# A hybrid attention layer with 32 experts: the output projection as three float32r passes

## The chip, the cores and the metric

The kernel runs as one program on one core of a Trainium2 chip. A core has TensorE (PE, matrix products; PEld is its loading of weights), VectorE (DVE), ScalarE (ACT), GpSimd (POOL) and SyncE (SP, which here issues most of the transfers), working memory of 128 partitions (SBUF), accumulators for products (PSUM), and 16 DMA engines that fetch from HBM. The metric is the device time of one execution in microseconds (us); lower is better.

## The reference

One layer on 256 rows of 1,024 channels, in float32. What surrounds the change, cut to its lines:

```python
merged = (gates[:, :, 0] * (y_a @ w_branch_a[l])
          + gates[:, :, 1] * (y_b @ w_branch_b[l])
          + gates[:, :, 2] * (y_c @ w_branch_c[l]))
mix = merged @ w_out[l]                                  # 256x1024 @ 1024x1024
x = _layer_norm(DEEPNORM_ALPHA * x + mix, ln1_g[l], ln1_b[l])
ffn = _moe(x, w_router[l], b_router[l], w_up[l], b_up[l], w_down[l], b_down[l])
x = _layer_norm(DEEPNORM_ALPHA * x + ffn, ln2_g[l], ln2_b[l])
```

`y_a`, `y_b`, `y_c` are the outputs of the attention, of the pooling and of the state space branch; all three and the gates come from one input projection `x @ w_in`. In `_moe` each row goes to 4 of 32 experts; an expert has 12 MB of weights, so that all of them are 384 MB.

## The kernel before, in words

Two parts follow each other. The **trunk** is everything up to the first layer norm and the router. The **experts** follow, two at a time, in 16 pairs of 24 weight chunks.

**The ring.** All large weights come through a ring of `NW` = 22 slots of 128x2048 float32 (1 MB each). Chunks 0 to 28 are the trunk's (`wt`), the 384 behind them the experts' (`wm`). A slot serves for other things too: the pieces of `x`, the gates (`gates0` to `gates2`), the branch outputs (`y`), `z` for the layer norm, and three slots `f_spl` for weights that are taken apart. `done` gives a chunk's slot back, `release` any other, and `load_more` (L109) at once writes a transfer of the next chunk into the program on SP's queue. SP carries these out in the order in which they were written: a transfer waits until its slot is free, and all behind it wait too. At most eight transfers are under way; a further one waits for the one eight places earlier. The ring is full when 22 slots are taken; it then loads no faster than the products give slots back.

**Three passes.** The products of the gates, of `v` and of the pooling input are done in float32r, which keeps part of a float32 number's bits. `split_next` takes a half chunk (128x1024) apart: ScalarE copies it rounded (`hi`, L233), VectorE subtracts (`lo`, L234). Then three products replace one in float32: hi by hi, hi by lo and lo by hi. The list `jobs` sets the order in which halves are taken apart, always up to three ahead, in the three slots `f_spl` in turn.

**The end of the trunk.** After the last gate product, `branch(d)` (d = 0 to 7) makes 128 of the 1,024 merged channels: eight float32 products of 256 columns (L768) into `pab` and `pcc`, then VectorE multiplies by the gates and adds (L777, L778, L782), and L783 writes `m`. `mixk` then adds channel block k to the output projection: four float32 products of 512 columns (L789), for two blocks of rows `t` and two halves of the columns `n`, into four accumulators `mix[t][n]` that gather over k. The weights of a branch pair and of an output pair come in chunks 21 to 28 in turn. The order on TensorE is written out in the code: `branch(k + 1)` stands ahead of `mixk(k)`, so that VectorE has a whole group of products' time for `m`:

```python
    branch(0)
    for k in range(7):
        branch(k + 1)
        if k < 6:
            mixk(*[(k, t, n) for t in range(2) for n in range(2)])
    mixk((6, 0, 0), (6, 0, 1), (6, 1, 0), (7, 0, 0), (7, 0, 1), (6, 1, 1), (7, 1, 0), (7, 1, 1))
```

(Left out there: small steps for the router between the groups.) Then L839 adds the residual to each accumulator, the rows are transposed (L851), and the router picks the experts (L866 to L952). The first product of an expert pair is L1037 (its bias), those with weights are L1028; `done` follows every four of them.

In a trace a float32 product shows as two records of TensorE, a float32r product as one.

Of the kernel before, what the change touches and what calls it, by code (L numbers as in the profile page):

```python
# [7 lines left out]
F32 = mybir.dt.float32  # L8
F32R = mybir.dt.float32r
BF16 = mybir.dt.bfloat16  # L10
I32 = mybir.dt.int32
ACTF = mybir.ActivationFunctionType
ALU = mybir.AluOpType
# [4 lines left out]
S = 256  # L18
# [36 lines left out]
CH_V = [6, 7]  # L55
CH_UP = 8
CH_G = list(range(9, 21))
CH_BR = [21, 23, 25, 27]
CH_WO = [22, 24, 26, 28]
N_TRUNK = 29  # L60


@with_exitstack
def hybrid_layer(ctx: ExitStack, tc: tile.TileContext, wt, wm, pa, pb, pc, xin, bu, lnp, b_down, out):
    nc = tc.nc
    pe, act, dve, pool, sp = nc.tensor, nc.scalar, nc.vector, nc.gpsimd, nc.sync
    TT, TS, STT = dve.tensor_tensor, dve.tensor_scalar, dve.scalar_tensor_tensor

    con = ctx.enter_context(tc.tile_pool(name="con", bufs=1))
# [5 lines left out]

    n_chunks = N_TRUNK + NP * 24
    chunks = {}
# [41 lines left out]
    def chunk(i):  # L119
        return chunks[i][0]  # L120

    def done(i):
        f = chunks.pop(i)[1]
        release(f)
# [17 lines left out]
    ones32 = con.tile([128, 32], F32)  # L142
    epst = con.tile([128, 2], F32)
    hpi = con.tile([128, 1], F32)
    junk = con.tile([128, 1], F32)


    ph1 = ExitStack()
# [55 lines left out]
    def drop(name):  # L204
        release(big.pop(name)[1])


    def gate_tile(i, n=1):
        return big[f"gates{i // 8}"][0].rearrange("p (u t) -> p u t", u=8)[:, i % 8:i % 8 + n]

    def yv(k, n=1):
        return big["y"][0].rearrange("p (k t) -> p k t", k=8)[:, k:k + n]
# [3 lines left out]

    SPLIT = CH_V + [CH_UP] + CH_G
    jobs = [(c, h) for c in SPLIT for h in range(2)]  # L220
    js = {"emitted": 0, "used": 0}
    parts = {}

    def split_next():
        j = js["emitted"]
        if j >= len(jobs):
            return
        js["emitted"] += 1
        ci, h = jobs[j]
        src = chunk(ci)[:, h * 1024:(h + 1) * 1024]  # L230
        t = place(f_spl[j % 3], F32R)
        hi, lo = t[:, 0:1024], t[:, 1024:2048]
        act.activation(out=hi, in_=src, func=ACTF.Copy)  # L233
        TT(lo, src, hi.bitcast(F32), op=ALU.subtract)  # L234
        parts[j] = (hi, lo)
        if h:
            done(ci)

    def split(ci, h):
        j = js["used"]  # L240
        js["used"] += 1
        assert jobs[j] == (ci, h)
        while js["emitted"] <= j:
            split_next()
        return parts.pop(j)

    def mm3(out, whi, wlo, ahi, alo, first, last):
        pe.matmul(out, whi, ahi, start=first, stop=False)  # L248
        pe.matmul(out, whi, alo, start=False, stop=False)  # L249
        pe.matmul(out, wlo, ahi, start=False, stop=last)  # L250
# [146 lines left out]


    def proj(ci, half, dst):
        if ci in SPLIT:  # L400
            hi, lo = split(ci, half)
            for k in range(8):
                mm3(dst, hi[:, k * 128:(k + 1) * 128], lo[:, k * 128:(k + 1) * 128], xhi[:, k], xlo[:, k], k == 0, k == 7)
            split_next()
        else:
            w = chunk(ci)[:, half * 1024:half * 1024 + 1024]
            for k in range(8):
                pe.matmul(dst, w[:, k * 128:(k + 1) * 128], xt3[:, k], start=(k == 0), stop=(k == 7))  # L408
            if half:
                done(ci)  # L410

    def pair_tile():
        return pm.tile([128, 2, S], F32, tag="m", name="pm")
# [190 lines left out]

    pus = pair_tile()
    proj(CH_US, 0, pus[:, 0])
    proj(CH_US, 1, pus[:, 1])
    act.activation(out=usT, in_=pus, func=ACTF.Copy)
    forget_logits()
# [131 lines left out]
    ph1.close()  # L741
    release(f_xhi)
    release(f_xlo)
    for f in f_spl:
        release(f)


    late = ctx.enter_context(tc.tile_pool(name="late", bufs=1, reuse_waits="tile"))
# [9 lines left out]
    wk2 = ps2.enter_context(tc.tile_pool(name="wk2", bufs=2, reuse_waits="tile"))  # L758
    mix = [[pmx.tile([128, 512], F32, name=f"mix{t}{n}") for n in range(2)] for t in range(2)]
    mst = {}  # L760

    def branch(d):
        w = chunk(CH_BR[d // 2])[:, d % 2 * 1024:d % 2 * 1024 + 1024]
        pab = pbr.tile([128, 2, S], F32, tag="ab", name="pab")
        pcc = pbr.tile([128, S], F32, tag="c", name="pcc")
        for dst, k0, k1 in ((pab[:, 0], 0, 4), (pab[:, 1], 4, 6), (pcc, 6, 8)):
            for k in range(k0, k1):
                pe.matmul(dst, w[:, k * 128:(k + 1) * 128], yv(k)[:, 0], start=(k == k0), stop=(k == k1 - 1))  # L768
        if d % 2:
            done(CH_BR[d // 2])  # L770

        t = wk2.tile([128, 3, S], F32, tag="mg", name="mg")
        if d == 5:
            STT(t[:, 0:1], gate_tile(15), 1.0, pab[:, 0:1], op0=ALU.add, op1=ALU.mult)
            STT(t[:, 1:2], gate_tile(16), 1.0, pab[:, 1:2], op0=ALU.add, op1=ALU.mult)
        else:
            STT(t[:, 0:2], gate_tile(3 * d, 2), 1.0, pab, op0=ALU.add, op1=ALU.mult)  # L777
        STT(t[:, 2:3], gate_tile(3 * d + 2), 1.0, pcc[:, None], op0=ALU.add, op1=ALU.mult)  # L778
        if d in (2, 5, 7):
            drop(f"gates{(d - 1) // 3 if d > 2 else 0}")  # L780
        m = wk2.tile([128, S], F32, tag="m", name="m", bufs=3)
        TT(t[:, 0], t[:, 0], t[:, 1], op=ALU.add)  # L782
        TT(m, t[:, 0], t[:, 2], op=ALU.add)  # L783
        mst[d] = m

    def mixk(*parts):
        for k, t, n in parts:
            w = chunk(CH_WO[k // 2])[:, k % 2 * 1024 + n * 512:k % 2 * 1024 + n * 512 + 512]
            pe.matmul(mix[t][n], mst[k][:, t * 128:(t + 1) * 128], w, start=(k == 0), stop=(k == 7))  # L789
            if (k % 2, t, n) == (1, 1, 1):  # L790
                done(CH_WO[k // 2])


    def router_weights():
# [15 lines left out]
    for k in range(7):  # L810
# [14 lines left out]
        if k < 6:  # L825
            mixk(*[(k, t, n) for t in range(2) for n in range(2)])
    mixk((6, 0, 0), (6, 0, 1), (6, 1, 0), (7, 0, 0), (7, 0, 1), (6, 1, 1), (7, 1, 0), (7, 1, 1))


    ps3 = ExitStack()  # L830
# [5 lines left out]
    for t in range(2):  # L836
        for n in range(2):
            ns = slice(n * 512, (n + 1) * 512)
# [57 lines left out]
    for t in range(2):  # L896
        for n in range(2):
            ns = slice(n * 512, (n + 1) * 512)
# [445 lines left out]
```

## Time and profile before

| | us |
|---|---|
| median of 3 runs | 1161.49 (1161.32 to 1161.6) |
| the profiled execution | 1161.53 |
| its span, first to last instruction | 1159.8 |
| TensorE busy | 1130.4 (97%) |
| TensorE's weight loads busy | 527.4 (45%) |
| VectorE busy | 300.9 (26%) |
| ScalarE busy | 184.7 (16%) |
| moved by DMA | 438.05 MB, mean 378 GB/s |

The profiled execution stands 0.04 us above the median, and 1.7 us of it lie outside the span. The busy share of TensorE is no measure of what bounds the kernel, since matmuls overlap and a matmul that waits for data in the pipeline counts as busy. The page's 40 slices of 29 us each show the moved GB/s over time; the views by stage show which engine waits for what.

### The profile page before, as it was taken

Reading aid. Unit: us, or ns where it says so; the run is one execution under the profiler, and the core shown is the slowest. Engines: PE = TensorE matmul, PEld = TensorE weight load, DVE = VectorE, ACT = ScalarE, POOL = GpSimd, SP = SyncE. Lnnn points to the kernel's source line nnn. Section 1 sums busy time; section 2 is a strip of 40 time slices with the busy share of each in tenths; the row PEclk is TensorE's granted clock in tenths of the full one; section 3 lists DMA queues with packets and bytes.
Section 4 is the critical chain, followed back from the end, with each engine's and each line's share of the span. In section 5 each row is a group of like instructions: output and inputs, shape, how many; then the busy total and the mean of one; then the engine's idle time right before and its main releaser. Section 6 shows DMA issues by size and latency. Waiting matters only on the chain. (4 is left out here: it accounts for less than half of the span.)

```text
span 1159.8 us, 13362 instructions
## 1 busy us (share of the span) xinstructions
PE 1130.4 (97%) x5535; PEld 527.4 (45%) x5535; DVE 300.9 (26%) x710; ACT 184.7 (16%) x389; POOL 13.5 (1%) x19
## 2 busy tenths in 40 slices
PE   9999999999999999999999999999999999999996
PEld 6888986643434343434343433343434344334332
DVE  4798622430202111111212121111111111111042
ACT  4555410310101010101010101010101010101002
POOL 0000000000000000000000000000000000000100
PEclk9999999999999999999999999999999999999999
DMA  9733685699999999999999999999999999999992
GB/s 368 306 110 137 243 358 212 253 423 421 420 421 421 421 421 421 421 421 420 421 422 420 421 421 420 414 422 420 422 421 420 422 420 421 421 421 420 420 412 87
DMA packets 63169, 438.05 MB, mean 378 GB/s; under 512 B 7136, under 2 KB 7648, under 8 KB 10752
## 3 DMA queue, kind: packets, MB, share of 16 engines
q1 hardware_dynamic: 62064, 435.46, 91.2%
q10 hardware_dynamic: 864, 1.54, 0.4%
q8 instruction: 45, 0.74, 0.3%
q0 software_dynamic: 176, 0.15, 0.0%
q14 instruction: 20, 0.16, 0.0%
HBM read 436.07 MB, written 1.05 MB: 377 GB/s over the span
## 5 line engine op out<-in xcount | busy, mean ns | idle before, releaser
L1028 PE MATMUL hu<-w,xg 128*64 128x512 f32 x2048 | 480.9, 596 | 14.2 <-DMA w<-in_wm_dram 14.2
L1028 PEld LDWEIGHTS hu<-w,xg 128*64 128x64 f32 x2048 | 166.0, 137 | 316.0 <-issue 262.1
L1028 PE MATMUL py<-w,at 128*64 128x512 f32 x1024 | 231.5, 597 | 0.0
L1000 DVE TENSOR_SCALAR s<-hu 128x256 f32<-128x256 f32 x64 | 27.0, 422 | 581.6 <-PE hu L1028 581.6
L1028 PEld LDWEIGHTS py<-w,at 128*64 128x64 f32 x1024 | 70.5, 136 | 136.0 <-issue 129.6
L1011 ACT ACTIVATE at<-pta 128x256 f32<-128x256 f32 x64 | 24.5, 383 | 422.9 <-PE pta L1010 422.9
L1037 PE MATMUL hu<-bup,pc_sb 128*64 128x512 f32 x256 | 68.3, 605 | 0.0
L1017 PE MATMUL acc<-y,gT 128*128 128x512 f32 x128 | 63.5, 618 | 1.5 <-ACT y L1045 1.5
L248 PE MATMUL pm<-w,w 128*128 128x256 f32 x208 | 60.6, 291 | 0.8 <-ACT vsb L641 0.8
L965 PE MATMUL pg<-oh,x 128*128 128x128 f32 x512 | 59.9, 275 | 0.0
L249 PE MATMUL pm<-w,w 128*128 128x256 f32 x208 | 58.8, 283 | 0.0
L250 PE MATMUL pm<-w,w 128*128 128x256 f32 x208 | 58.8, 282 | 0.0
L965 PEld LDWEIGHTS pg<-oh,x 128*128 128x128 f32 x512 | 58.4, 192 | 0.1
L1001 ACT ACTIVATE hu<-s 128x256 f32<-128x256 f32 x64 | 24.6, 385 | 168.3 <-DVE s L1000 168.3
L1045 ACT ACTIVATE y<-py 128x512 f32<-128x512 f32 x32 | 19.1, 597 | 190.9 <-PE py L1028 190.9
L234 DVE TENSOR_TENSOR w<-w,w 128x1024 fp32r<-128x1024 f32 x30 | 36.5, 1219 | 19.3 <-ACT w L233 19.1
L248 PEld LDWEIGHTS pm<-w,w 128*128 128x128 f32 x208 | 39.7, 191 | 3.8 <-issue 1.7
L1017 PEld LDWEIGHTS acc<-y,gT 128*128 128x128 f32 x128 | 21.7, 189 | 42.9 <-issue 39.7
L249 PEld LDWEIGHTS pm<-w,w 128*128 128x128 f32 x208 | 39.8, 191 | 0.1
L250 PEld LDWEIGHTS pm<-w,w 128*128 128x128 f32 x208 | 39.8, 191 | 0.0
L233 ACT ACTIVATE w<-w 128x1024 fp32r<-128x1024 f32 x30 | 31.6, 1057 | 35.3 <-PE pm L250 25.1
L408 PE MATMUL pm<-w,w 128*128 128x256 f32 x160 | 36.1, 383 | 1.1 <-DMA w<-in_wt_dram 1.1
(320 smaller groups left out, 681.8 us busy)
## 6 DMA issues: line engine op xcount, KB each, us to landing
w<-in_wm_dram SPq DMA_DIRECT2D x382, 1024.0 KB, 19.8
w<-in_wt_dram SPq DMA_DIRECT2D x26, 1024.0 KB, 7.9
w<-in_wm_dram SPq DMA_DIRECT2D x8, 256.0 KB, 11.7
w<-in_wt_dram SPq DMA_DIRECT2D x4, 256.0 KB, 5.6
w<-in_wt_dram ACTq DMA_DIRECT2D x4, 256.0 KB, 5.9
w<-in_wt_dram SPq DMA_DIRECT2D x2, 512.0 KB, 5.0
w<-in_xin_dram SPq DMA_DIRECT2D x1, 1024.0 KB, 7.7
w<-in_pb_dram SPq DMA_DIRECT2D x1, 896.0 KB, 8.5
```

What stands on the lines that cost most here:

```text
L233: act.activation(out=hi, in_=src, func=ACTF.Copy)
L234: TT(lo, src, hi.bitcast(F32), op=ALU.subtract)
L248: pe.matmul(out, whi, ahi, start=first, stop=False)
L249: pe.matmul(out, whi, alo, start=False, stop=False)
L250: pe.matmul(out, wlo, ahi, start=False, stop=last)
L408: pe.matmul(dst, w[:, k * 128:(k + 1) * 128], xt3[:, k], start=(k == 0), stop=(k == 7))
L965: pe.matmul(pg[:, b], x1[:, t, k * 128:(k + 1) * 128], oh[:, t], start=(t == 0), stop=(t == 1))
L1000: TS(xg, hu[:, 0:256], 7.0, None, op0=ALU.min)
L1001: act.activation(out=th, in_=xg, func=ACTF.Tanh, scale=0.851)
L1017: pe.matmul(accs[t][n], gT[:, t * 128:(t + 1) * 128], y, start=first, stop=True, skip_group_check=True)
L1028: pe.matmul(dst[64 * e:64 * e + 64], lhs[:, k, 64 * e:64 * e + 64], w[:, k % 4], start=first and k == 0, stop=(k == 7))
L1037: pe.matmul(hu[64 * e:64 * e + 64], ident[:, i:i + 1].to_broadcast([128, 64]), bup, start=True, stop=False)
```

## The change

The output projection's weights (chunks 22, 24, 26, 28) join the list `jobs`, behind those of the gates, so that `split_next` takes their eight halves apart too. `branch` no longer writes `m`: it adds in place, ScalarE copies the sum rounded to `mh` (128x256, float32r) and VectorE subtracts to `ml`. `mixk` does three float32r products for each of its float32 products, and calls `split_next` after the last of a block. A chunk's slot now goes back when its second half has been taken apart (`half_done`), not when it has been multiplied. The three slots `f_spl`, which went back after the gates, go back after the last `mixk`. Last, a tile of 96 bytes takes the place of one of 4 (which took 32), ahead of the ring: in the built program the ring starts at byte 20,416 of a partition before, and at 20,480 = 20 x 1,024 now. The branch products stay in float32 (the loop's `d in ()` holds for none).

```diff
-    junk = con.tile([128, 1], F32)
+    scr = con.tile([128, 24], F32)
+    junk = scr[:, 0:1]
...
-    SPLIT = CH_V + [CH_UP] + CH_G
-    jobs = [(c, h) for c in SPLIT for h in range(2)]
+    jobs = [(c, h) for c in CH_V + [CH_UP] + CH_G for h in range(2)]
+    for d in range(8 + LAG):
...
+        if d - LAG in (0, 1, 2, 3, 4, 5, 6, 7):
+            jobs.append((CH_WO[(d - LAG) // 2], (d - LAG) % 2))
...
+    def half_done(ci):
+        halves[ci] = halves.get(ci, 0) + 1
+        if halves[ci] == 2:
+            done(ci)
...
-    for f in f_spl:
-        release(f)
...
-        m = wk2.tile([128, S], F32, tag="m", name="m", bufs=3)
         TT(t[:, 0], t[:, 0], t[:, 1], op=ALU.add)
-        TT(m, t[:, 0], t[:, 2], op=ALU.add)
-        mst[d] = m
+        if (CH_WO[d // 2], d % 2) in jobs:
+            mh = wk2.tile([128, S], F32R, tag="mh", name="mh", bufs=3)
+            ml = wk2.tile([128, S], F32R, tag="ml", name="ml", bufs=3)
+            TT(t[:, 0], t[:, 0], t[:, 2], op=ALU.add)
+            act.activation(out=mh, in_=t[:, 0], func=ACTF.Copy)
+            TT(ml, t[:, 0], mh.bitcast(F32), op=ALU.subtract)
+            mst[d] = mh, ml
...
     def mixk(*parts):
         for k, t, n in parts:
-            w = chunk(CH_WO[k // 2])[:, k % 2 * 1024 + n * 512:k % 2 * 1024 + n * 512 + 512]
-            pe.matmul(mix[t][n], mst[k][:, t * 128:(t + 1) * 128], w, start=(k == 0), stop=(k == 7))
-            if (k % 2, t, n) == (1, 1, 1):
-                done(CH_WO[k // 2])
...
+                if k not in ws:
+                    ws[k] = split(ci, h)
+                hi, lo = ws[k]
+                pe.matmul(mix[t][n], m[:, ts], hi[:, ns], start=(k == 0), stop=False)
+                pe.matmul(mix[t][n], m[:, ts], lo[:, ns], start=False, stop=False)
+                pe.matmul(mix[t][n], ml[:, ts], hi[:, ns], start=False, stop=(k == 7))
+                if (t, n) == (1, 1):
+                    split_next()
...
+    for j in (3, 2, 1):
+        release(f_spl[(len(jobs) - j) % 3])
```

Three places show what moves. On **TensorE** at block k = 3, between `branch(4)` and `branch(5)` (names: accumulator <- weights in their slot, merged rows), before:

```order
L768 MATMUL pcc_1748<-w5_411,w14_1154 128x256 x2
L789 MATMUL mix00_1657<-w17_1152,m_1740 128x512
L789 MATMUL mix01_1658<-w17_1152,m_1740 128x512
L789 MATMUL mix10_1659<-w17_1152,m_1740 128x512
L789 MATMUL mix11_1660<-w17_1152,m_1740 128x512
L768 MATMUL pab_1770<-w5_411,w14_1154 128x256 x6
```

and now:

```order
L832 MATMUL mix00_1662<-w12_1718,mh_1777 128x512
L833 MATMUL mix00_1662<-w12_1718,mh_1777 128x512
L834 MATMUL mix00_1662<-w12_1718,ml_1778 128x512
L832 MATMUL mix01_1663<-w12_1718,mh_1777 128x512
L833 MATMUL mix01_1663<-w12_1718,mh_1777 128x512
L834 MATMUL mix01_1663<-w12_1718,ml_1778 128x512
L832 MATMUL mix10_1664<-w12_1718,mh_1777 128x512
L833 MATMUL mix10_1664<-w12_1718,mh_1777 128x512
L834 MATMUL mix10_1664<-w12_1718,ml_1778 128x512
L832 MATMUL mix11_1665<-w12_1718,mh_1777 128x512
L833 MATMUL mix11_1665<-w12_1718,mh_1777 128x512
L834 MATMUL mix11_1665<-w12_1718,ml_1778 128x512
```

The weights now come from one of the three slots `f_spl` (w12), not from the chunk's own (w17), and each accumulator is written three times in a row. What stands around the block is the same.

On **VectorE** at the last block, d = 7, where L839 (L886 now) adds the residual, before:

```order
L777 SCALAR_TENSOR_TENSOR mg_1834<-w9_1331,pab_1822 128x512
L778 SCALAR_TENSOR_TENSOR mg_1834<-w9_1331,pcc_1823 128x256
L782 TENSOR_TENSOR mg_1834<-mg_1834 128x256
L783 TENSOR_TENSOR m_1839<-mg_1834 128x256
L839 SCALAR_TENSOR_TENSOR w8_1712,sums_1854<-w8_1712,mix00_1657 128x512
```

and now:

```order
L799 SCALAR_TENSOR_TENSOR mg_1923<-w9_1331,pab_1911 128x512
L800 SCALAR_TENSOR_TENSOR mg_1923<-w9_1331,pcc_1912 128x256
L803 TENSOR_TENSOR mg_1923<-mg_1923 128x256
L807 TENSOR_TENSOR mg_1923<-mg_1923 128x256
L809 TENSOR_TENSOR ml_1930<-mg_1923,mh_1929 128x256
L886 SCALAR_TENSOR_TENSOR w8_1736,sums_1966<-w8_1736,mix00_1662 128x512
```

Between L807 and L809 stands a copy on ScalarE (`mh`), for which VectorE's queue waits.

On **SP's queue**, the last transfers of expert chunks before the first that takes the slot of an expert chunk (w_2101 before, w_2213 now), with what each waits for, before:

```order
L109 DMA w_1820<-in_wm_dram 128x2048 [waits DMAHW3_49,PE_49]
L109 DMA w_1832<-in_wm_dram 128x2048 [waits DMAHW4_49,PE_49]
L109 DMA w_1837<-in_wm_dram 128x2048 [waits DMAHW5_49,DVE_49,Activation_49]
L109 DMA w_1842<-in_wm_dram 128x2048 [waits DMAHW6_49]
L109 DMA w_1852<-in_wm_dram 128x2048 [waits DMAHW7_49,PE_49]
L109 DMA w_1988<-in_wm_dram 128x2048 [waits DVE_49,PE_49,DMAHW0_49,Activation_49,Pool_49]
L109 DMA w_2101<-in_wm_dram 128x2048 [waits DMAHW1_49,PE_49]
```

and now:

```order
L111 DMA w_1921<-in_wm_dram 128x2048 [waits DMAHW2_49,PE_49]
L111 DMA w_1926<-in_wm_dram 128x2048 [waits DMAHW3_49,DVE_49]
L111 DMA w_1934<-in_wm_dram 128x2048 [waits DMAHW4_49]
L111 DMA w_1960<-in_wm_dram 128x2048 [waits DMAHW5_49]
L111 DMA w_1962<-in_wm_dram 128x2048 [waits DMAHW6_49,PE_49]
L111 DMA w_1964<-in_wm_dram 128x2048 [waits DMAHW7_49,PE_49]
L111 DMA w_2100<-in_wm_dram 128x2048 [waits DVE_49,PE_49,DMAHW0_49,Activation_49,Pool_49]
L111 DMA w_2213<-in_wm_dram 128x2048 [waits DMAHW1_49,PE_49]
```

Before, the four ahead of the last two go into the slots of chunks 26 and 27, of `gates2` and of `y`, the next into chunk 28's, the last into that of `z`. Now it is chunk 27's, `gates2`, `y`, then the three `f_spl` (w_1960 to w_1964), then `z`: from chunk 27's on these are seven where there were five, since the slots `f_spl` have not gone back after the gates, and chunk 28's has gone back already.

## Rows read from the trace of the kernel before

**Rows 1.** The page: span, and GB/s moved in 40 equal slices

```profile
span 1159.8 us, 13362 instructions
...
GB/s 368 306 110 137 243 358 212 253 423 421 420 421 421 421 421 421 421 421 420 421 422 420 421 421 420 414 422 420 422 421 420 422 420 421 421 421 420 420 412 87
```

**Rows 2.** By stretch: length, busy of each engine, PE clock, DMA share, GB/s

```profile
156.40:211.70 55.30, 55.30 (x196) 36.64 (x195) 18.43 (x43) 3.44 (x6) 1.23 (x2) 1.00 0.73 288
211.70:221.90 10.20, 9.87 (x142) 8.86 (x140) 7.14 (x31) 6.22 (x12) 1.54 (x2) 1.00 0.80 308
221.90:228.70 6.80, 6.80 (x39) 3.12 (x39) 2.27 (x10) 1.83 (x4) 0.00 (x0) 1.00 0.00 0
228.70:630.00 401.30, 401.30 (x1896) 149.19 (x1892) 69.14 (x170) 42.30 (x102) 0.00 (x0) 1.00 1.01 420
630.00:1136.60 506.60, 489.81 (x2158) 192.60 (x2157) 85.41 (x199) 50.74 (x120) 7.70 (x9) 1.00 1.01 418
```

**Rows 3.** Waits for DMA (total us, times, longest): 228.7 to 630, then 630 to 1137

```profile
PEld hu L1028 <- DMA w<-in_wm_dram: 0.8, 3, 0.3
...
PEld hu L1028 <- DMA w<-in_wm_dram: 38.3, 36, 2.2
...
SPq L109 <- DMA w<-in_wm_dram: 407.9, 193, 3.6
```

**Rows 4.** Timeline (start, length, engine, line): first product of pairs 0, 4, 5, 14, 15

```profile
223.22 0.65 PE L1037 MATMUL hu<-bup,pc_sb 128*64 128x512 f32 x2
...
439.73 0.60 PE L1037 MATMUL hu<-bup,pc_sb 128*64 128x512 f32 x2
...
494.37 0.60 PE L1037 MATMUL hu<-bup,pc_sb 128*64 128x512 f32 x2
...
1021.43 0.60 PE L1037 MATMUL hu<-bup,pc_sb 128*64 128x512 f32 x2
...
1081.09 0.60 PE L1037 MATMUL hu<-bup,pc_sb 128*64 128x512 f32 x2
```

**Rows 5.** Timeline, SP: transfers of expert chunks around the end of the trunk

```profile
205.03 1.29 SPq L109 DMA_DIRECT2D w<-in_wm_dram  x3
...
217.28 0.33 SPq L109 DMA_DIRECT2D w<-in_wm_dram  x1
...
227.76 0.33 SPq L109 DMA_DIRECT2D w<-in_wm_dram  x1
```

**Rows 6.** Timeline, PE: one block of the projection, the last two, the transposes

```profile
170.18 3.60 PE L789 MATMUL mix<-w,m 128*128 128x512 f32 x8
...
173.61 2.75 PE L768 MATMUL pab<-w,w 128*128 128x256 f32 x12
...
204.84 7.03 PE L789 MATMUL mix<-w,m 128*128 128x512 f32 x16
...
211.70 1.91 PE L851 MATMUL tpx<-pc_sb,w 128*128 128x128 f32 x16
```

**Rows 7.** Timeline, PE: float32r products of 512 columns for `v`

```profile
50.45 0.39 PE L634 MATMUL pv<-w,w 128*128 128x512 f32 x1
50.67 0.40 PE L635 MATMUL pv<-w,w 128*128 128x512 f32 x1
...
53.18 0.39 PE L634 MATMUL pv<-w,w 128*128 128x512 f32 x1
```

**Rows 8.** The page's groups: busy, mean ns of one, idle before

```profile
L1011 ACT ACTIVATE at<-pta 128x256 f32<-128x256 f32 x64 | 24.5, 383 | 422.9 <-PE pta L1010 422.9
...
L234 DVE TENSOR_TENSOR w<-w,w 128x1024 fp32r<-128x1024 f32 x30 | 36.5, 1219 | 19.3 <-ACT w L233 19.1
...
L233 ACT ACTIVATE w<-w 128x1024 fp32r<-128x1024 f32 x30 | 31.6, 1057 | 35.3 <-PE pm L250 25.1
```

**Rows 9.** Timeline, ACT and DVE: gaps at the last gates, and the last merged rows

```profile
156.58 0.60 ACT L739 ACTIVATE w<-pm 128x512 f32<-128x512 f32 x1 [5.16 <-PE pm L250]
...
159.18 0.69 DVE L777 SCALAR_TENSOR_TENSOR mg<-w,pab 128x512 f32<-128x512 f32 x1 [8.92 <-PE pab L768]
...
205.83 0.42 DVE L783 TENSOR_TENSOR m<-mg 128x256 f32<-128x256 f32 x1
```

More of the change, by code (lines that the diff above doesn't have):

```diff
@@ L60 @@
 N_TRUNK = 29
+LAG = 1
 @with_exitstack
@@ L215, in work @@
         return place(f).rearrange("p (i q t) -> p i q t", i=4, q=2)
-    SPLIT = CH_V + [CH_UP] + CH_G
-    jobs = [(c, h) for c in SPLIT for h in range(2)]
+    jobs = [(c, h) for c in CH_V + [CH_UP] + CH_G for h in range(2)]
+    for d in range(8 + LAG):
+        if d in ():
+            jobs.append((CH_BR[d // 2], d % 2))
+        if d - LAG in (0, 1, 2, 3, 4, 5, 6, 7):
+            jobs.append((CH_WO[(d - LAG) // 2], (d - LAG) % 2))
     js = {"emitted": 0, "used": 0}
     parts = {}
+    halves = {}
+    def half_done(ci):
+        halves[ci] = halves.get(ci, 0) + 1
+        if halves[ci] == 2:
+            done(ci)
     def split_next():
@@ L235, in split_next @@
         parts[j] = (hi, lo)
-        if h:
-            done(ci)
+        half_done(ci)
     def split(ci, h):
@@ L399, in proj @@
     def proj(ci, half, dst):
-        if ci in SPLIT:
+        if (ci, half) in jobs:
             hi, lo = split(ci, half)
@@ L408, in proj @@
                 pe.matmul(dst, w[:, k * 128:(k + 1) * 128], xt3[:, k], start=(k == 0), stop=(k == 7))
-            if half:
-                done(ci)
+            half_done(ci)
     def pair_tile():
@@ L762, in branch @@
     def branch(d):
-        w = chunk(CH_BR[d // 2])[:, d % 2 * 1024:d % 2 * 1024 + 1024]
+        ci, h = CH_BR[d // 2], d % 2
+        exact = (ci, h) in jobs
+        if exact:
+            hi, lo = split(ci, h)
+        else:
+            w = chunk(ci)[:, h * 1024:h * 1024 + 1024]
         pab = pbr.tile([128, 2, S], F32, tag="ab", name="pab")
@@ L767, in branch @@
             for k in range(k0, k1):
-                pe.matmul(dst, w[:, k * 128:(k + 1) * 128], yv(k)[:, 0], start=(k == k0), stop=(k == k1 - 1))
-        if d % 2:
-            done(CH_BR[d // 2])
+                ks = slice(k * 128, (k + 1) * 128)
+                if exact:
+                    mm3(dst, hi[:, ks], lo[:, ks], yh(k)[:, 0], yl(k)[:, 0], k == k0, k == k1 - 1)
+                else:
+                    pe.matmul(dst, w[:, ks], yv(k)[:, 0], start=(k == k0), stop=(k == k1 - 1))
+        if exact:
+            split_next()
+        else:
+            half_done(ci)
         t = wk2.tile([128, 3, S], F32, tag="mg", name="mg")
@@ L780, in branch @@
             drop(f"gates{(d - 1) // 3 if d > 2 else 0}")
-        m = wk2.tile([128, S], F32, tag="m", name="m", bufs=3)
         TT(t[:, 0], t[:, 0], t[:, 1], op=ALU.add)
-        TT(m, t[:, 0], t[:, 2], op=ALU.add)
-        mst[d] = m
+        if (CH_WO[d // 2], d % 2) in jobs:
[5 more added lines that the diff above has]
+            mst[d] = mh, ml
+        else:
+            m = wk2.tile([128, S], F32, tag="m", name="m", bufs=3)
+            TT(m, t[:, 0], t[:, 2], op=ALU.add)
+            mst[d] = m, None
+    ws = {}
     def mixk(*parts):
         for k, t, n in parts:
-            w = chunk(CH_WO[k // 2])[:, k % 2 * 1024 + n * 512:k % 2 * 1024 + n * 512 + 512]
-            pe.matmul(mix[t][n], mst[k][:, t * 128:(t + 1) * 128], w, start=(k == 0), stop=(k == 7))
-            if (k % 2, t, n) == (1, 1, 1):
-                done(CH_WO[k // 2])
+            ci, h = CH_WO[k // 2], k % 2
+            ts, ns = slice(t * 128, (t + 1) * 128), slice(n * 512, (n + 1) * 512)
+            m, ml = mst[k]
+            if ml is None:
+                w = chunk(ci)[:, h * 1024:h * 1024 + 1024]
+                pe.matmul(mix[t][n], m[:, ts], w[:, ns], start=(k == 0), stop=(k == 7))
+                if (t, n) == (1, 1):
+                    half_done(ci)
+            else:
+                if k not in ws:
[4 more added lines that the diff above has]
+                pe.matmul(mix[t][n], ml[:, ts], hi[:, ns], start=False, stop=(k == 7))
+                if (t, n) == (1, 1):
+                    split_next()
     def router_weights():
```

## The prediction

> **What bounds the kernel now.** I read the page's slices first: from the ninth slice on, some 230 us into the span, the moved GB/s stand at some 421 nearly to the end, and ahead of that they go up and down [rows 1]. So the question is where the kernel is bound by this stream of expert weights and where by TensorE. The table by stretch answers it. From 228.7 to 1136.6 us the stream runs without a gap, 1.01 of the DMA engines' time, and just ahead of it the engines move nothing for 6.8 us [rows 2]. That idle is a full ring: the next transfer leaves at 227.76, when the first products of the experts give two slots back, while the one ahead of it left at 217.28 [rows 5].
>
> After that, TensorE and the stream run beside each other. Up to 630 us TensorE waits for weights 0.8 us in all, after it 38.3 us in 36 waits, and SP's queue itself waits for earlier transfers to land, 193 times [rows 3]. The starts of the pairs say the same: 54.64 us from pair 4 to 5 (494.37 - 439.73), where TensorE sets the pace, and 59.66 us from pair 14 to 15, where the stream is [rows 4]. One pair is 24 chunks of 1,048,576 bytes, and 25.17 MB at 421 GB/s are 59.8 us. So the end is bound like this: the stream starts for good when TensorE reaches the first expert products, it runs 908 us (1136.6 - 228.7), and a tail of 23.2 us follows it to the end of the span at 1159.8 [rows 1, 2].
>
> A faster trunk moves the end only by what it moves that start. All of the gain counts if the ring is full by then, none beyond. And what TensorE does after some 630 us costs nothing.
>
> **The products.** A block of the projection (four float32 products, eight records) takes 3.43 us, from 170.18 to the next branch at 173.61 [rows 6]. The nearest row for what takes its place is the same shape in the same type, the `v` products: stationary 128x128, moving 512 columns, three passes with the first two on the same stationary operand. From 50.45 to 53.18 are twelve of them, 2.73 us, 0.2275 each [rows 7]. A block is then 12 x 0.2275 = 2.73 us, and 3.43 - 2.73 = 0.70 us are saved; for eight blocks, 5.6 us. Bounds from the same stretch: the first spacing shown there is 0.22, which would make 2.64 and 6.3 us in all; the whole starts I see are rounded to 0.01, and the wide end for a slow start of each block, 0.24, gives 2.88 and 4.4 us. I take 5.6, as the mean over twelve.
>
> Here the Trainium skill says something else. Its page FP8 and Floating Point Precision (TensorE Precision Notes) has a true float32 product as four passes through the array. By that, three passes would save a quarter of 3.43 us a block, 6.9 us in all, an estimate from that page, and the kernel would take 1154.7. The rows say a fifth, since three passes of 0.2275 us stand against 0.86 us for a float32 product; the sum goes by the rows.
>
> **Taking apart.** Eight halves cost ScalarE 1.06 and VectorE 1.22 us each, and eight merged rows 0.38 (a copy of 128x256) and about 0.43 us (the subtraction has the shape of L783, 0.42) [rows 8, 9]. That is 11.5 us on ScalarE and 13.2 on VectorE, and I cost it at nothing but for the last block. What hides it: in the 55.3 us of branches and projection VectorE is busy 18.4 and ScalarE 3.4 us [rows 2]. Three halves are taken apart during the last gates, where ScalarE had been idle 5.16 us ahead of its last copy and VectorE 8.92 us ahead of the first merge [rows 9]. The other five follow one each behind blocks 0 to 4, when the slot that they write comes free. A half needs 1.06 + 1.22 = 2.3 us and is used three blocks later, and a block with its branch will take 6.2 us: block 1 begins at 170.18 and block 6 at 204.84 [rows 6], 34.66 / 5 = 6.9 us apart, less 0.70. From the end of a block to the next branch's first result are 2.75 us [rows 6], so the merge on VectorE doesn't queue behind the half either, by some 0.4 us; if it does, the merged rows still have a whole block's time before they are used.
>
> On ScalarE's queue, the halves stand ahead of the gates' last two tanh copies. `branch(0)` and `branch(1)` reuse the accumulators that these read. The last tanh stood at 156.58; behind a half it comes about 1.1 us later, 158.3 at its end, and `branch(1)` starts one branch (6.9 - 3.43 = 3.5 us) after `branch(0)` at 156.4, at 159.9. If this cover were gone, it would cost what tanh is late, at most 1 us. The table load for the square root moves in between blocks 4 and 5 on ScalarE; what stands behind it, half 7, is used last of all.
>
> **The last block.** It alone has little cover. Before, the last merged rows are ready at 206.25, 1.41 us after the last two blocks begin at 204.84 [rows 6, 9]. Now `mh` follows 0.38 us and a hop later, at 1.85, and `ml` at 2.3. The products of k = 6 that stand ahead take nine passes, 2.05 us, and `ml` is first read two passes later, at 2.50. Both are in time by 0.2 us. Bounds: 0 to 0.5 us of stall. I take 0.1. What follows, from the accumulators to the first layer norm, keeps its form; its last addition waits for the last product, then as now.
>
> **The ring.** Two moves count on SP's queue. Chunks 24, 26 and 28 go back when taken apart, two to three blocks earlier than when multiplied. The three slots `f_spl` go back after the projection, at 202 to 206 us in place of 157. So the queue's last seven transfers before the restart bunch up: chunk 27's slot, `gates2`, `y` and one `f_spl` from 205.03 - 6 x 0.70 = 200.8 on, the second `f_spl` near 204.8, the third at 206.1, `z` at 217.28 - 5.5 = 211.8 [rows 5]. All ahead of them has landed by about 197, since the last half is taken apart behind block 4 (204.84 - 2 x 6.9 - 4 x 0.70 + 2.73 + 2.3 = 193.3), and chunk 28's slot goes back with it. Seven transfers of 2.49 us (1.049 MB at 421 GB/s) end at 200.8 + 1 + 17.4 = 219.2. The restart is due at 228.7 - 5.5 = 223.2. The ring is then full 4.0 us ahead of it, where it was 6.8 us [rows 2], so that the whole gain goes through. Another 4 us off the trunk would not.
>
> **The address.** A shift of 64 bytes costs no instruction. The 908 us stream writes into these slots, so each per cent of its speed is 9.1 us. No row shows another address, so this has no bound from rows but the floor that TensorE's own pairs set: 223.22 + 15 x 54.64 = 1042.8 for the last pair, 38.3 us ahead of 1081.09 [rows 4]. On the other side nothing excludes a loss. The rate is nearly the same in all slices of the stream [rows 1], whichever of the 22 slots is written; but all of them have the same offset, so this tells nothing of the shift. I take 0, since no row speaks for a sign, and allow 0.1% of the stream, 0.9 us, either way in the forecast's own range.
>
> **The sum.** 1161.53 (the profiled execution, 0.04 above the median) - 5.6 + 0.1 = **1156.0 us**.
>
> **Rivals.** First, **the stream gets faster**. A row that starts off a grid of the memory touches one piece more of it than one that starts on it, and 20,480 is a multiple of more powers of two than 20,416. If time goes by pieces, each per cent is 9.1 us, up to TensorE's floor at 38.3; I give it the middle, 19 us, 1137. The Trainium skill has such a rule in DMA: Bandwidth & Descriptors (How a descriptor splits into AXI transactions): a descriptor goes in pieces of 256 bytes, and one that doesn't start at a multiple of 256 costs beats for the bytes below its start. By that figure a row of 8,192 bytes would go from 33 pieces to 32, which by my estimate is 908 / 33 = 27.5 us and 1128.5. The page speaks of what is fetched, and here it is the written side that shifts; no run here shows either. For the rival: the stream is what the end hangs on, without a gap. Against it: no row in which the rate varies with where it writes. Chance 0.10.
>
> Second, and slower than before: **the stream gets slower** by the same shift, all 16 engines now starting their rows at the same 1 KB boundary. From 0.6% on (5.5 us of 908) it eats the gain; at 1% the kernel takes 1165.1. For it speaks only that no row shows the new address, against it that the rate is flat beside very different loads of the other engines [rows 2]. Chance 0.03.
>
> Third, **the ring is late**. If the transfers from 200.8 on slip by over 4.0 us, the restart is no longer TensorE's, and each further us is lost; at 9.6 us nothing is left and the kernel takes 1161.5. The queue is in order, so one late slot would do it. Each of those slots, though, is released by a product that I have placed. Chance 0.03, around 1159.
>
> Fourth, **TensorE waits for the parts** in each block, 0.3 us on the average: 2.4 us, 1158.4. For it: six pieces of work share VectorE's queue in a block where four did. Against: 6.2 us a block hold 18.4 / 8 + 1.22 + 0.43 = 4.0 us of VectorE's work. Chance 0.03.
>
> That float32r doesn't save at all is out by the `v` rows.
>
> **How the numbers follow.** The forecast has 0.81, with 1156.0. Its range: the fast spacing gives 1155.2 and the slow one with 0.5 us of stall 1157.6, so -0.8 and +1.6; with the stream's 0.9 either way, as independent errors, -1.2 and +1.8, thus 1154.8 to 1157.8. The rivals outside it are 0.19 together, so the range stays there. A measurement of this kernel can tell 0.2%, 2.3 us. Faster: forecast, first and fourth, 0.94. Same: the third, 0.03. Slower: the second, 0.03.
>
> **What would show it.** In the profile after: L832 to L834 with starts 0.227 us apart; transposes near 206.2 where they were at 211.70; the first L1037 near 217.7 where it was at 223.22 [rows 4, 6]; an idle gap of DMA of about 4 us that ends near 223.2; then some 421 GB/s without a gap, pairs of 59.66 us at the end, and the same tail. The forecast is wrong if the stream's rate moves, if the gap is gone, or if TensorE stands still ahead of L832.

## The result

The changed kernel takes 1145.22 us (median of 4 runs, 1144.18 to 1146.05) against 1161.55 for the kernel before (4 runs, 1161.32 to 1162.25). The ratio is 0.9858, with a 95% interval of 0.9841 to 0.9875. That is 16.3 us less. The prediction had 5.5 us less, 1156.0, with a range down to 1154.8, so it was wrong: faster, as it said, but by three times as much, and most of the gain came from the edit that it had costed at nothing.

The profiled execution took 1145.35 us. The first lines to read are the same as before, the page's span and its slices of GB/s:

```profile
span 1143.5 us, 13471 instructions
...
GB/s 373 312 97 131 242 330 237 315 422 426 427 427 426 426 426 427 427 427 426 427 427 427 425 426 428 422 426 427 426 428 426 428 426 427 426 427 426 426 414 85
```

Where the slices stood at 421 all through the stream of expert weights [rows 1], they stand at 427. It isn't one stretch that got faster, it is the whole stream. The table by stretch (length; busy time and count of TensorE, weight loads, VectorE, ScalarE, GpSimd; clock; DMA share; GB/s) has 424 and 423 where [rows 2] had 420 and 418:

```profile
222.70:630.00 407.30, 407.30 (x1924) 151.18 (x1922) 71.44 (x176) 43.05 (x103) 0.00 (x0) 1.00 1.01 424
630.00:1120.90 490.90, 481.00 (x2134) 182.64 (x2131) 83.59 (x193) 50.00 (x118) 7.70 (x9) 1.00 1.01 423
1120.90:1143.50 22.60, 14.80 (x45) 4.53 (x43) 8.12 (x17) 4.26 (x8) 2.86 (x2) 0.91 0.13 49
```

The stream now ends at 1120.9 where it ended at 1136.6 [rows 2]. Its share of the DMA engines' time is 1.01 in both kernels: by this measure the engines were never idle there, before or now. The same share of time moves more bytes, and this is what the share alone can't tell.

Behind the stream, the tail is 22.6 us (23.2 before). TensorE waits less for weights after 630 us, as it must when they come faster (us in all, times, longest; [rows 3] had 38.3 in 36, counted from 600 us on; from 630 it is 38.1 in 35):

```profile
PEld hu L1075 <- DMA w<-in_wm_dram: 27.9, 28, 1.8
```

The other part of the gain lies ahead of the stream. The transposes behind the projection start at 206.56 where they started at 211.70 [rows 6], and the first expert product at 218.08 where it was 223.22 [rows 4]; both are 5.14 us earlier. The queue gives out the first transfer of the stream at 222.61, where it was 227.76 [rows 5]. The timeline (start, length, engine, line) of TensorE, then of SP:

```profile
206.56 1.91 PE L898 MATMUL tpx<-pc_sb,w 128*128 128x128 f32 x16
...
218.08 1.08 PE L1084 MATMUL hu<-bup,pc_sb 128*64 128x512 f32 x4
```

```profile
222.61 1.67 SPq L111 DMA_DIRECT2D w<-in_wm_dram  x2
```

So there are two gains, about 5 us in the trunk and about 11 in the stream. The change has two edits that could each be the cause of the second: the ring's new address, and the three passes, which also change when VectorE and ScalarE work and when slots come free. The first experiments take them apart.

### The profile page after: what moved, and what is told of

The parts are those of the page before. It is cut to its first block, busy times and chain, and to the rows that moved or that the text cites. A ratio compares the mean times of both kernels' runs of the same rounds, so it can differ in the third digit from the quotient of the medians.

```text
span 1143.5 us, 13471 instructions
## 1 busy us (share of the span) xinstructions
PE 1121.9 (98%) x5567; PEld 525.6 (46%) x5567; DVE 314.2 (27%) x726; ACT 196.1 (17%) x405; POOL 14.4 (1%) x19
## 5 line engine op out<-in xcount | busy, mean ns | idle before, releaser
L1075 PEld LDWEIGHTS hu<-w,xg 128*64 128x64 f32 x2048 | 156.6, 137 | 314.7 <-issue 280.4
L262 PE MATMUL pm<-w,w 128*128 128x256 f32 x208 | 60.6, 292 | 0.8 <-ACT vsb L654 0.8
L263 PE MATMUL pm<-w,w 128*128 128x256 f32 x208 | 58.8, 283 | 0.0
L264 PE MATMUL pm<-w,w 128*128 128x256 f32 x208 | 58.8, 283 | 0.0
L249 DVE TENSOR_TENSOR w<-w,w 128x1024 fp32r<-128x1024 f32 x38 | 46.3, 1220 | 32.2 <-ACT w L248 32.1
L248 ACT ACTIVATE w<-w 128x1024 fp32r<-128x1024 f32 x38 | 40.0, 1057 | 44.9 <-PE pm L264 30.2
L1016 ACT ACTIVATE xg<-pg,pc_sb 128x128 f32<-128x128 f32 x64 | 29.3, 457 | 48.1 <-DVE xg L1018 48.1
```

Source lines behind the costliest of these rows:

```text
L1016: act.activation(out=xg[:, k], in_=pg[:, b], func=ACTF.Identity, scale=l1[:, k:k + 1], bias=l1[:, 8 + k:9 + k])
L1075: pe.matmul(dst[64 * e:64 * e + 64], lhs[:, k, 64 * e:64 * e + 64], w[:, k % 4], start=first and k == 0, stop=(k == 7))
```

## Experiments

**The address alone.** The kernel before, with the ring moved by 64 bytes to 20,480:

```diff
-    junk = con.tile([128, 1], F32)
+    scr = con.tile([128, 24], F32)
+    junk = scr[:, 0:1]
```

> The kernel before with the ring moved by 64 B to 20480, and nothing else: the projection stays in float32 and no part of it is taken apart. Theory (the start address of the ring sets the rate of the saturated stream): the stream still restarts at 228.7 us, its 907.9 us shrink by the 1.07% seen in the changed kernel, 9.7 us, the tail by 0.5, so about 1151.3 us, and the slices of the page read 427 GB/s where they read 421. Rival (the three passes change the stream, by taking VectorE's and ScalarE's phase against the transfers elsewhere or by freeing the slots differently): 1161.5 us and 421 GB/s.

Measured: 1149.59 us (median of 10) against 1161.78, ratio 0.9921 with an interval of 0.9894 to 0.9949. Seven runs lie at 1149.0 to 1150.1 and three at 1155.6, 1160.3 and 1161.3, which makes the interval wide. The same kernel once more:

> The kernel before with the ring at 20480, as in the first experiment. If the three runs of ten there that lay at 1155.6 to 1161.3 us belong to this kernel, some of these lie there too; if not, all lie within 1149.0 to 1150.4 us, as the eight runs with the ring at 256 and 512 B above did (1148.6 to 1150.4).

Four runs on another chip, all at 1149.0 to 1149.6, median 1149.17, ratio 0.9890 (0.9874 to 0.9907). The three odd runs didn't come back, and nothing here says what they were. The table by stretch of the first of the two:

```profile
228.60:630.00 401.40, 401.40 (x1896) 149.12 (x1892) 69.08 (x170) 42.38 (x102) 0.00 (x0) 1.00 1.01 426
630.00:1124.40 494.40, 484.69 (x2157) 182.77 (x2157) 85.05 (x199) 50.54 (x120) 7.88 (x9) 0.99 1.01 424
```

The stream starts where it did, at 228.6, with the same work of the engines beside it (1896 products, 401.40 us of TensorE), and it moves 426 and 424 GB/s where it moved 420 and 418 [rows 2]. That is 1.4%, and it ends 12.2 us earlier. The address alone does it. The rival is out: the projection of this kernel is untouched. It is 1.7 us faster than the theory expected, which had taken 1.07% from the whole stream of the changed kernel; that stream also has a slow start, which comes up again below and accounts for part of it.

**The change without the address.** The other half: the changed kernel with `junk` as it was, and so the ring at 20,416.

```diff
-    scr = con.tile([128, 24], F32)
-    junk = scr[:, 0:1]
+    junk = con.tile([128, 1], F32)
```

> The changed kernel with the ring left at 20416, the three passes and the taking apart kept. Theory: the restart of the stream comes 6.0 us earlier as in the changed kernel (222.7 us), the stream runs at 421 GB/s, so 1161.5 - 6.0 = 1155.5 us, inside the range that was predicted for this part alone. Rival: 1145.2 us, since the passes bring it all.

Measured: 1157.59 us (5 runs, 1156.32 to 1158.04), ratio 0.9964 (0.9949 to 0.9978), and 421 GB/s in the page's slices: 12 us from the rival, and 2 us above what the theory expected. Over the same 300 us in the middle of the stream, this kernel and the one with the address alone:

```profile
300.00:600.00 300.00, 300.00 (x1426) 113.19 (x1424) 50.14 (x124) 33.51 (x79) 0.00 (x0) 1.00 1.01 421
```

```profile
300.00:600.00 300.00, 300.00 (x1426) 113.17 (x1422) 52.29 (x129) 33.69 (x80) 0.00 (x0) 1.00 1.01 427
```

The three passes bring 4.2 us by the medians (5.2 in the profiled run, which was the fastest of the five), the address 12.2 to 12.7. Together that is 16.4 to 16.9, against the 16.3 of the whole change (17.1 in its repeat below); the two edits add up within the spread of the runs. And 1157.6 lies in the range that the prediction gave for its own case, near its upper end.

**Which grid.** The change puts the ring at a multiple of 1 KB. Four more kernels, all like the first one but with another width of `scr` (32, 56, 88 and 152 columns), put the ring at 32, 128, 256 and 512 bytes above 20,480.

> The kernel before with the ring at 20512, 32 B above a multiple of 1 KB. If the cost is one of being off the grid at all: 1161.5 us, as for 64 B off. If it grows as the start gets odder (an element of the grid of 64 B cut in two at each piece): slower than before, by the 2% that the next step of the same size would be, 1171 us.

> The kernel before with the ring at 20608, 128 B above a multiple of 256. If it is enough that the start is a multiple of 128 B: 1151.3 us as with 20480. If the grid that counts is 256 B (the Trainium skill, DMA: Bandwidth & Descriptors, How a descriptor splits into AXI transactions, cuts a row at each 256 B) or coarser: 1161.5 us as at 20416.

> The kernel before with the ring at 20736, 256 B above a multiple of 1 KB. Theory (the grid is 256 B, as the Trainium skill's page DMA: Bandwidth & Descriptors cuts rows): 1149.6 us and 427 GB/s, as at 20480. Rival (the grid is 512 B or 1 KB, as the change's own words have it): 1161.6 us and 421 GB/s, as at 128 B off.

> The kernel before with the ring at 20992, 512 B above a multiple of 1 KB. With a grid of 256 or of 512 B: 1149.6 us and 427 GB/s. With a grid of 1 KB: 1161.6 us and 421 GB/s. A row is 8192 B, so a start on 512 B cuts it in 16 pieces of 512 B just as a start on 1 KB does.

| ring above a multiple of 1 KB | median us | ratio to before | GB/s, 300 to 600 us |
|---|---|---|---|
| 0 B (the second set) | 1149.17 (4) | 0.9890 | 427 |
| 32 B | 1164.92 (10) | 1.0026 | 419 |
| 128 B | 1161.58 (10) | 0.9998 | 421 |
| 256 B | 1149.54 (4) | 0.9897 | 427 |
| 512 B | 1149.59 (4) | 0.9896 | 427 |
| 960 B (the kernel before) | 1161.8 | 1 | 421 |

Two rows of that last column, for 128 and for 256 bytes:

```profile
300.00:600.00 300.00, 300.00 (x1428) 113.32 (x1424) 52.29 (x129) 33.69 (x80) 0.00 (x0) 1.00 1.01 421
```

```profile
300.00:600.00 300.00, 300.00 (x1428) 113.22 (x1424) 52.25 (x129) 33.71 (x80) 0.00 (x0) 1.00 1.01 427
```

The kernel before, at 960, lies 192 bytes above a multiple of 256. Of the starts tried, a multiple of 256 bytes is all that is needed; 128 is not enough, and 512 or 1 KB bring nothing more. A start at 32 bytes costs a further 0.3% (its interval is 1.0017 to 1.0036), not the 2% that I had as the other case. This grid is the one that the Trainium skill gives in DMA: Bandwidth & Descriptors (How a descriptor splits into AXI transactions): a descriptor goes in pieces of 256 bytes, and a start off that grid costs. The page speaks of what is fetched, and here it is the written side that moved; the runs show the same grid there. They do not agree with the size that I had estimated from the page, one piece in 33, 3%: they have 1.4%.

**The stream by itself.** Is it the transfer that gets dearer, or does an odd row only collide with the engines that read beside it? This kernel leaves the computation out; it loads 32 MB at each offset, first with idle engines, then with TensorE and ScalarE reading each slot and VectorE copying the products. There is one run of it.

```diff
+    for busy in range(2):
+        for off in OFFSETS:
+            o = off // 4
+            for _ in range(LOADS):
+                t = ring.tile([128, 2304], F32, tag=f"w{n % SLOTS}", name=f"w{n % SLOTS}")
+                c = n % 384
+                sp.dma_start(out=t[:, o:o + 2048], in_=wm[c // 12, c % 12])
...
```

> The computation is left out: twelve stretches of 32 loads of 1 MB each into 20 slots of SBUF, with the slots at 0, 64, 32, 128, 256 and 512 B above a multiple of 1 KB; six stretches with all engines idle, then the same six with TensorE reading two 512-column products of each slot and VectorE and ScalarE a copy each. Theory (a row that starts off the grid costs the transfer itself more): in the idle half already 427 GB/s at 0 and 421 at 64 and 128, 419 at 32. Rival (the odd piece costs only where engines read or write the same memory): the same rate at every offset in the idle half, and a difference in the busy half alone.

The table by stretch; the first six rows are the idle half, at 0, 64, 32, 128, 256 and 512 bytes, the last four the busy half at 0, 64, 32 and 128:

```profile
10.00:80.00 70.00, 0.00 (x0) 0.00 (x0) 0.00 (x0) 0.00 (x0) 0.00 (x0) 1.00 1.01 428
86.00:160.00 74.00, 0.00 (x0) 0.00 (x0) 0.00 (x0) 0.00 (x0) 0.00 (x0) 1.00 1.01 422
166.00:240.00 74.00, 0.00 (x0) 0.00 (x0) 0.00 (x0) 0.00 (x0) 0.00 (x0) 1.00 1.01 420
246.00:320.00 74.00, 0.00 (x0) 0.00 (x0) 0.00 (x0) 0.00 (x0) 0.00 (x0) 1.00 1.01 422
326.00:398.00 72.00, 0.00 (x0) 0.00 (x0) 0.00 (x0) 0.00 (x0) 0.00 (x0) 1.00 1.01 428
404.00:476.00 72.00, 0.00 (x0) 0.00 (x0) 0.00 (x0) 0.00 (x0) 0.00 (x0) 1.00 1.01 427
484.00:556.00 72.00, 57.85 (x120) 20.44 (x119) 20.74 (x30) 8.98 (x29) 0.00 (x0) 1.00 1.01 427
562.00:636.00 74.00, 58.31 (x120) 20.33 (x120) 20.43 (x30) 9.30 (x30) 0.00 (x0) 1.00 1.01 422
642.00:716.00 74.00, 57.83 (x119) 20.14 (x120) 20.09 (x30) 9.08 (x30) 0.00 (x0) 1.00 1.01 420
722.00:796.00 74.00, 58.38 (x120) 20.32 (x120) 20.42 (x30) 9.30 (x30) 0.00 (x0) 1.00 1.01 422
```

With all engines idle the rates are already those of the kernels: 428 on the grid, 422 at 64 and 128 bytes, 420 at 32. TensorE busy for 58 of 74 us changes none of them. So the cost lies in the transfer: it is there in full with nothing else at work on the core. It also shows that 427 to 428 is the most that this kind of transfer reaches here: the kernel's stream, with all its waits and engines, runs as fast as one with nothing beside it.

**Shorter rows.** If each row costs one more piece, shorter rows should lose more. The same idle stream, in rows of 8, 4 and 2 KB (1, 2 and 4 transfers for a slot), each at 0, 64 and 32 bytes, in one run:

> The computation is left out: nine stretches of 32 MB each into 20 slots of SBUF with all engines idle, in rows of 8, 4 and 2 KB, each at 0, 64 and 32 B above a multiple of 1 KB. Theory (the cost is one per row, for the one more piece in which a row off the grid of 256 B is cut): the loss at 64 B grows from 1.3% at 8 KB to 2.6% at 4 KB and 5.2% at 2 KB. Rival (the cost is one per piece of 256 B, or per byte): 1.3% at each length of row.

The table by stretch (this kernel's program has only VectorE and GpSimd in it, so two columns of busy time), with three rows for 4 KB (0, 64 and 32 bytes) and two for 2 KB (0 and 64):

```profile
248.00:320.00 72.00, 0.00 (x0) 0.00 (x0) 1.00 1.03 419
328.00:404.00 76.00, 0.00 (x0) 0.00 (x0) 1.00 1.03 410
410.00:486.00 76.00, 0.00 (x0) 0.00 (x0) 1.00 1.03 409
492.00:570.00 78.00, 0.00 (x0) 0.00 (x0) 1.00 1.05 390
578.00:658.00 80.00, 0.00 (x0) 0.00 (x0) 1.00 1.04 383
```

At 64 bytes the loss is 1.4% at 8 KB (428 to 422, here as in the run above), 2.1% at 4 KB and 1.8% at 2 KB. So it is more for shorter rows, but it doesn't double with each halving, and neither of the two theories fits. What one odd row costs in itself, and by what mechanism, stays open. Shorter rows, with more transfers for a slot, are slower by themselves: on the grid the rates are 428, 419 and 390.

**The changed kernel again.**

> The changed kernel as it is, once more beside the kernel before. Of ten runs of the kernel before with the ring at 20480 three fell out of the group (1155.6, 1160.3 and 1161.3 us against 1149.0 to 1150.1). If that is a property of the aligned stream, some of the runs here lie near 1155 us, the time of the change without the address; if it came from that one kernel, all lie within 1144 to 1146.

Four runs at 1143.86 to 1144.81, median 1144.65, ratio 0.9853 (0.9837 to 0.987). None near 1155.

**Does each microsecond of the trunk count?** The prediction's step on the ring said that the transfers run dry ahead of the restart, and that another 4 us off the trunk would not go through. Two of three passes test it; the product with the low part of the weights is left out.

```diff
                 pe.matmul(mix[t][n], m[:, ts], hi[:, ns], start=(k == 0), stop=False)
-                pe.matmul(mix[t][n], m[:, ts], lo[:, ns], start=False, stop=False)
                 pe.matmul(mix[t][n], ml[:, ts], hi[:, ns], start=False, stop=(k == 7))
```

> The changed kernel without the second of the three passes (the merged rows times the low parts of the weights); this part of the projection is left out. It takes 32 passes of 0.233 us, 7.5 us, out of the trunk. Theory (the prediction's step on the ring: the transfers before the restart run out and the flow of bytes stands still, in the changed kernel from 220.0 us to about 224 us, and TensorE's time counts only as far as that): about 4 us faster than the changed kernel, 1140.6 us, with no stretch at a low rate between 206 us and 1116 us. Rival (each microsecond of TensorE ahead of the restart counts in full): 1144.7 - 7.5 = 1137.2 us.

Measured: 1138.12 us (4 runs, 1137.55 to 1138.71), 6.5 us less than the repeat of the changed kernel (1144.65) and 7.1 less than its first four runs (1145.22). The rival, 7.5 us, was nearer than the theory, 4. The stretches around the restart, first of the changed kernel, then of this one:

```profile
216.00:220.00 4.00, 4.00 (x30) 2.73 (x30) 2.04 (x7) 1.80 (x4) 0.00 (x0) 1.00 1.01 426
220.00:224.00 4.00, 4.00 (x22) 1.29 (x18) 0.58 (x4) 0.03 (x1) 0.00 (x0) 1.00 0.16 33
224.00:230.00 6.00, 6.00 (x30) 2.01 (x28) 1.70 (x4) 0.39 (x1) 0.00 (x0) 1.00 0.95 336
```

```profile
208.00:214.00 6.00, 6.00 (x44) 4.45 (x46) 2.39 (x9) 1.83 (x4) 0.00 (x0) 1.00 1.00 419
214.00:218.00 4.00, 4.00 (x22) 1.32 (x20) 0.23 (x2) 0.00 (x0) 0.00 (x0) 1.00 0.27 68
218.00:224.00 6.00, 6.00 (x30) 2.01 (x28) 1.70 (x4) 0.39 (x1) 0.00 (x0) 1.00 0.99 412
```

The idle stretch is still there, 6 us earlier, at 33 GB/s in the one and 68 in the other. It hardly shrank, because the slots of those last transfers are given back by the projection itself, and a shorter projection sends them out earlier too. SP's timeline shows it: the last three transfers before the restart leave at 199.03, 199.96 and 206.00 where they left at 205.35, 206.75 and 212.14, and the restart comes at 216.22 where it was at 222.61. The transposes are 6.8 us earlier (199.76 for 206.56), not 7.5. Part of what is missing is in the last blocks, where TensorE now waits for the copy of the merged rows (0.4 us, once):

```profile
PE mix L832 <- ACT mh L808: 0.4, 1, 0.4
```

**How much cover the taking apart has.** Each half of the weights is taken apart twice:

```diff
-        act.activation(out=hi, in_=src, func=ACTF.Copy)
-        TT(lo, src, hi.bitcast(F32), op=ALU.subtract)
+        for _ in range(2 if ci in CH_WO else 1):
+            act.activation(out=hi, in_=src, func=ACTF.Copy)
+        for _ in range(2 if ci in CH_WO else 1):
+            TT(lo, src, hi.bitcast(F32), op=ALU.subtract)
```

> The changed kernel with each taking apart of the projection's weights done twice: 8 more copies of 1.22 us on ScalarE and 8 more subtractions of 1.06 us on VectorE, with the same outputs. Theory (the taking apart lies beside TensorE's work with room to spare): 1144.7 us, within 0.5, and the transposes still at about 206.5 us. Rival (the parts are just in time, and the 0.4 us by which the trunk's saving came short are TensorE waiting for them): the transposes later by 0.5 us a block or more, 1149 us.

(The two durations in that text stand the wrong way round: the copy has 1.06 and the subtraction 1.22 us [rows 8].) Measured: 1146.85 us (4 runs, 1145.98 to 1147.79), 2.2 us more than the repeat of the changed kernel and 1.6 more than its first four runs, between the two expectations. TensorE's waits and its line ahead of the last two blocks:

```profile
PE mix L834 <- ACT mh L810: 0.8, 2, 0.5
```

```profile
200.62 1.03 PE L790 MATMUL pcc<-w,w 128*128 128x256 f32 x4
202.19 0.50 PE L834 MATMUL mix<-w,mh 128*128 128x512 f32 x1 [0.54 <-ACT mh L810]
```

The last two blocks begin 1.57 us after the start of the branch's last products, where 0.68 is the rule (next section). The transposes start at 208.42 and the stream restarts at 224.47, both 1.86 us later than in the changed kernel. In the changed kernel itself no wait of TensorE for `mh` or `ml` is in the profile. So the taking apart is hidden as it stands, but a second one of the same size no longer is.

## Why the prediction was wrong, point by point

**What bounds the kernel** held: the stream from the restart to the end, then the tail. Its consequence, that each per cent of the stream's rate is 9.1 us, held too: 1.4% would be 12.7, and the address alone brought 12.2 to 12.7. (The 0.8 us of waits up to 630 are those of one line; the same view has 1.5 us more for the products into `py`, which changes nothing.)

**The address** is the step that failed. The prediction took it as 0, since no row speaks for a sign, and allowed 0.9 us. It measured 12 us. The effect was there as the first rival, with a chance of 0.10: rows that start off a grid. A grid there is, of 256 bytes, but the size was wrong: 19 us as a middle value, 27.5 by the estimate from the page's pieces, and 12 in the runs. That one more piece per row is the cause isn't shown; the shorter rows speak against a fixed cost per row. The argument against it was that the rate never varies with where the stream writes. But as the prediction says in the same part, all 22 slots had the same offset, so this was no evidence; a value of 0 with 0.9 us of bounds was drawn from it all the same. With nothing that bounds the step from rows, the range had to reach to that rival.

**The products.** Predicted 0.70 us a block, 5.6 in all; the trunk became 5.14 us shorter. The first line is of the kernel before, the others of the changed one:

```profile
169.32 1.03 PE L768 MATMUL pcc<-w,w 128*128 128x256 f32 x4
```

```profile
168.58 1.03 PE L788 MATMUL pcc<-w,w 128*128 128x256 f32 x4
169.26 0.58 PE L832 MATMUL mix<-w,mh 128*128 128x512 f32 x1
169.68 0.39 PE L833 MATMUL mix<-w,mh 128*128 128x512 f32 x1
169.91 0.39 PE L834 MATMUL mix<-w,ml 128*128 128x512 f32 x1
...
172.01 0.39 PE L834 MATMUL mix<-w,ml 128*128 128x512 f32 x1
172.24 0.59 PE L788 MATMUL pab<-w,w 128*128 128x256 f32 x2
```

The block takes 2.98 us (169.26 to 172.24), not 2.73. Its first pass behind a float32 product holds the next one back by 0.42 us, the other eleven take 0.233 and not 0.2275 (172.24 - 169.68 = 2.56, over 11). But the block also begins 0.68 us after the start of the branch's last group of products, where it was 0.86 (169.32 to 170.18 [rows 6]), and these 0.18 us make up for what the first pass loses against 0.233. Together 4.29 us became 3.66, so 0.63 a block and 5.0 in all. What is short of 5.6 us is thus mostly the 0.005 us by which each pass is slower than the mean of the `v` rows; the prediction's bounds, 4.4 to 6.3, hold it. So the signs that the prediction had named came a little late: passes 0.233 apart where it had 0.227, transposes at 206.56 for 206.2, the first expert product at 218.08 for 217.7. The `v` passes were the right row for the shape. The twelve of them that were counted stand behind passes of their own kind, so what happens at the start of a block wasn't in them; that the two sides of it cancel was luck.

**Taking apart** at nothing held, shown by the absence of waits and by the doubled version, which cost 1.6 to 2.2 us. **The last block** held closely. Predicted were `mh` and `ml` in time by 0.2 us. The timeline of the changed kernel has the first passes of k = 7 on TensorE, and the last `ml` and `mh` on VectorE and ScalarE:

```profile
203.05 0.39 PE L832 MATMUL mix<-w,mh 128*128 128x512 f32 x1
...
203.52 0.40 PE L834 MATMUL mix<-w,ml 128*128 128x512 f32 x1
```

```profile
202.90 0.43 DVE L809 TENSOR_TENSOR ml<-mg,mh 128x256 fp32r<-128x256 f32 x1 [0.54 <-ACT mh L808]
```

```profile
202.45 0.42 ACT L808 ACTIVATE mh<-mg 128x256 fp32r<-128x256 f32 x1 [5.84 <-DVE mg L807]
```

`mh` is there at 202.87 and read at 203.05, `ml` at 203.33 and read at 203.52: 0.18 and 0.19 us. Counted from the start of the two blocks, at 200.75, all four come some 0.25 us later than forecast (`mh` at 2.12 for 1.85 and read at 2.30 for 2.05), so that the margin held partly by luck.

**The ring** held for this change: the seven transfers were to end at 219.2 and the engines to stand idle for 4.0 us; they run at 426 GB/s to 220.0 and at 33 to 224.0. Its last sentence, that another 4 us off the trunk would not go through, was wrong, as the two passes showed: of another 7.5 us, 6.5 to 7.1 went through, since the bunched transfers hang on the projection as well. After the restart the changed kernel moves only 336 GB/s for six us (224 to 230, above); against 427 that is some 1.3 us. The repeat of the changed kernel has it too (344), but neither half of the change does: the change without the address moves 392 in the same six us, and the address alone 395 and the kernel before 388 in theirs (229 to 235). So it was seen only with both edits together, and not in the kernel with two passes either (412 from 218 to 224); its cause stays open.

**The other rivals.** The stream didn't get slower on the 1 KB boundary, the ring wasn't late, and no wait of TensorE for the parts is in the profile.

The profiled runs, added up: the restart's first transfer 5.15 us earlier (227.76 to 222.61); the stream from there to its end 908.8 us (1136.6 - 227.76) against 898.3 (1120.9 - 222.61), so 10.5 less; the tail 0.6 less. That is 16.3 us, as measured. With the address alone the stream takes 896.7 us (1124.4 - 227.68); of the 1.6 us between that and 898.3, some 0.8 are the slow start (336 for 395 GB/s over six us).

## What to carry to other kernels

Where a kernel hangs on a long stream into SBUF, look at the start address of its buffers within a row of memory first: a small tile allocated ahead of the ring decides it, and padding that tile cost 64 bytes of each partition here and no instruction. A flat rate in the profile says only that nothing varies; it is no evidence that the rate can't be higher, and an edit for which no row gives a bound must widen the range, not be set to zero. A saving of TensorE's time ahead of a wait can go through even where the transfers run dry in front of it, if the slots of those transfers are released by the same work: here nearly all of another 7.5 us did.

## What the runs showed of the hardware

- Transfers of 128 rows of 8 KB into SBUF ran at 427 to 428 GB/s when the rows began at a multiple of 256 bytes, at 421 to 422 at 64, 128 or 192 bytes above one, and at 419 to 421 at 32 bytes above one (192 in the kernel alone, 64 in the stream alone, the others in both); the stream alone has the same rates with idle and with busy engines. That a shift of 64 bytes would be worth 1% of the whole kernel had been given a chance of 0.10.
- The share of the DMA engines' time reads 1.01 in all of these cases of 8 KB rows. A saturated queue looks the same at either rate, and only the bytes moved tell them apart.
- A float32r pass of 512 columns right behind the branch's float32 products delays its successor by 0.42 us, where the following ones are 0.233 apart. The first pass of the last block, which stands behind float32r passes, is followed after 0.23 us (203.05 to 203.28). So the delay belongs to what stands ahead of the pass; that it is the change of type isn't shown.
